# A fp32 Hymba layer on one core: four sums split as one buffer, six more seven-product quads, and output rows finished one pair later

## The chip, the cores and the metric

The kernel runs on one core of a Trainium2 chip. The metric is device time in microseconds (us) of one execution. The kernel before takes 1720.13 us, the median of 3 runs (1720.1 to 1720.97). Engines are named as the profile names them: PE does matrix products, DVE and ACT work on vectors, SP issues most transfers; PEld is PE's weight load and POOL is almost unused.

## The reference

`x` is 256 tokens by 4096, everything is fp32, and there is one layer.

```python
u = rmsnorm(x, norm_gain)
q, k, v, z_a, hc, b_gate, c_gate, z_c = split(u @ w_in)      # 8 x 2048 columns
attn = moba_attention(q, k, v, rel_bias) * silu(z_a)         # 16 heads of 128, causal;
                                # 256 tokens are one block, so each token sees its own block
conv = b_gate * short_conv(c_gate * hc, conv_w) * silu(z_c)  # causal, width 3
h = x + concatenate([attn, conv]) @ w_out                    # 4096 x 4096
return rmsnorm(h, final_gain)
```

## The kernel before, in words

**Pairs and quads.** The columns of `w_in` (16384) and `w_out` (4096) are cut into chunks of 512. Two chunks make a pair: pairs 0 to 15 are the input projection, 16 to 19 the output projection. The 4096 rows that a pair sums over are cut into 16 quads of 256 rows. A quad is one 1 MB tile `raw` (128 x 2048: two row blocks times two chunks), used with two token tiles of 128.

**Exact products.** Each fp32 operand is split in a high part (a cast on ACT, L540) and a low part (a subtraction on DVE, L542). A block of 128 x 128 x 512 is three matmuls: L607 and L608 (both parts of `x` with `hi`) and L610 (the high part of `x` with `lo`).

**Eight or seven products.** A plain quad is 8 blocks, 24 matmuls, and its `hi` and `lo` are split from `raw` directly. A "seven" quad uses a Strassen-like scheme of 7 blocks, 21 matmuls. For it DVE first adds blocks of weights into a tile `sum` (L521 1024 wide, L522 and L523 512 wide). Three blocks are split from `raw` (1536 wide), four from `sum` (two units of 1024). The operand of such a quad has 7 parts (8 for quad 14) rather than 4, so its `x` must be summed too (L150 to L152). How many sevens a pair has is given by a letter in `KIND` and, for pairs 0, 1 and 16, by a set. In all 141 of the 320 quads are sevens.

**Order of issue.** The units of all quads (one for a plain quad, three for a seven) are walked in order. Ahead of the matmuls of unit u the splits of unit u+2 are issued (`split`), and with the first unit of a quad the load of the quad two ahead. `hi` and `lo` have 3 buffers each, `raw` has 3. Each engine runs its instructions in the order of issue. So a DVE instruction that waits holds up all splits behind it.

**Accumulators.** Seven of the eight PSUM banks are in use in a pair: 1, 5, 6 and 7 belong to sevens alone and are added together after the last seven quad (`early`, `out_early`); 2, 3, 4 and 8 run to the end of the pair and are finished in `two_done` or `out_end`. In output pairs `out_early` adds into the residual rows `hg` at once, and `out_end` adds the rest, squares it on ACT and multiplies by the final gain `gf`, per 512 columns. In pairs 10, 12 and 14 the short convolution (`conv`) runs between the matmuls behind the last seven quad; it turns tiles on PE and sums on DVE.

**The end.** In pair 19 the `hi` and `lo` of the last three quads are kept, so that token tile 0 (banks 4 and 8) is finished first. `finish(0)` scales and stores it while PE works on banks 3 and 2 of token tile 1; `finish(1)` follows.

**The start.** Twelve matmuls on zeros (`WARM`) fill PE until the first operands are there.

Of the kernel before, what the change touches and what calls it, by code (L numbers as in the profile page):

```python
# [17 lines left out]
P = 128  # L18
# [12 lines left out]
WARM = 12  # L31
# [3 lines left out]
KIND = "01888888" "8n7n7n7n" "077e"  # L35
RING = 3
SLOT = 4
LO = 4
HI = 2
TS = (5, 7, 9, 11)  # L40
# [19 lines left out]
FIRST = (1, 3, 5, 7, 0, 9, 2, 11, 4, 8, 6, 10, 13, 12, 14, 15)  # L60
USUAL = tuple(range(16))
# [18 lines left out]
def of(pattern):  # L80
# [9 lines left out]
RAISE = {(1, 1): 4, (1, 3): 6, (1, 12): 0, (1, 13): 2, (1, 15): 14,  # L90
# [8 lines left out]
def hymba_layer(ctx: ExitStack, tc: tile.TileContext, xT, xres, gain, w, convw, wout,  # L99
# [15 lines left out]
    ss = const.tile([P, 2, 2 * NDP], F32, name="ss")  # L115
# [54 lines left out]
    def x_parts(q, xr):  # L170
        dst = operands(q)
        if q in SEVENS[0]:
            c = x_scaled(q, xr)
            sums_of(c)
            parts(dst, c[:, :7])
            return
# [12 lines left out]
    def m_parts(q, c):  # L189
        dst = operands(q)  # L190
        if q in SEVENS[N_PAIRS]:
            sums_of(c)
            parts(dst, c[:, :7])
        else:
            parts(dst[:, :4], c[:, :4])

    def made_up(q, c):
        sums_of(c)
        parts(A[q][:, 4:7], c[:, 4:7])
        g = 7 if q == BOTH else 0  # L200
        parts(A[q][:, g:g + 1], c[:, :1])
# [8 lines left out]
    def rsqrt(dst, ps, n):  # L210
# [6 lines left out]
        nc.vector.tensor_tensor(s, dst, dst, ALU.mult)  # L217
        nc.vector.tensor_tensor(s, s, v, ALU.mult)
# [122 lines left out]
    def conv(k, n):  # L341
# [8 lines left out]
        y = cur["pool"].tile([P, S], F32, name="y", bufs=2)  # L350
# [9 lines left out]
    ENDS = ((3, 1, 1, "v"), (2, 1, 0, "e"), (4, 0, 0, "u"), (8, 0, 1, "w"))  # L360

    def early(acc):

        e, v, u, w_ = (ep.tile([P, B], F32, name=f"e{i}") for i in range(4))
        nc.scalar.copy(e, acc[1])
        nc.vector.tensor_tensor(v, acc[6], e, ALU.add)  # L366
        nc.vector.tensor_tensor(u, acc[7], v, ALU.add)
        nc.vector.tensor_tensor(v, acc[5], v, ALU.subtract)
        nc.vector.tensor_tensor(w_, acc[5], u, ALU.subtract)
        return {"e": e, "v": v, "u": u, "w": w_}  # L370

    def scaled(es, rows):

        for _, t, n, name in ENDS:
            nc.scalar.activation(es[name], es[name], AF.Copy, scale=rows[n][:, t:t + 1])
# [52 lines left out]
    def row_of(p, t, n):  # L428
        c = 2 * p + n
        return fin["hg"][:, t, c * B:(c + 1) * B]  # L430

    def out_early(p, acc):
        v, u = (ep.tile([P, B], F32, name=f"e{i}") for i in range(2))
        x11, x12, x21, x22 = row_of(p, 1, 0), row_of(p, 1, 1), row_of(p, 0, 0), row_of(p, 0, 1)
        nc.scalar.copy(v, acc[1])
        nc.vector.tensor_tensor(x11, x11, v, ALU.add)
        nc.vector.tensor_tensor(v, acc[6], v, ALU.add)
        nc.vector.tensor_tensor(u, acc[7], v, ALU.add)
        nc.vector.tensor_tensor(v, acc[5], v, ALU.subtract)
        nc.vector.tensor_tensor(x12, x12, v, ALU.add)  # L440
        nc.vector.tensor_tensor(x21, x21, u, ALU.add)
        nc.vector.tensor_tensor(u, acc[5], u, ALU.subtract)
        nc.vector.tensor_tensor(x22, x22, u, ALU.add)
        gain_load(p)

    def out_end(p, ts=(1, 0), accs=(2, 3, 4, 8)):
        for b_, t, n, _ in ENDS:
            if t not in ts or b_ not in accs:
                continue
            hh = row_of(p, t, n)  # L450
            nc.vector.tensor_tensor(hh, cur["acc"][b_], hh, ALU.add)  # L451
            sq = ep.tile([P, B], F32, name=f"e{2 + n}")
            nc.scalar.activation(sq, hh, AF.Square, accum_out=ss[:, t, 2 * p + n:2 * p + n + 1])  # L453
            nc.vector.tensor_tensor(hh, hh, fin["gf"][:, n * B:(n + 1) * B], ALU.mult)  # L454

    def finish(t):
# [16 lines left out]
    def load(n):  # L473
# [33 lines left out]
    def split(u):  # L507
# [28 lines left out]
        step = B if n < LEAD else m if m < 4 * B else LO * B  # L536
# [9 lines left out]
    def tasks_of(p):  # L546
# [207 lines left out]
```

## Time and profile before

| | before |
|---|---|
| median of 3 runs | 1720.13 us |
| the profiled execution's own time | 1719.89 us |
| its span | 1718.1 us |
| mean granted clock of PE | 0.997 of full speed |
| PE busy | 1701.9 us (99%), 7639 matmuls |
| DVE busy | 1532.2 us (89%), 1534 instructions |
| ACT busy | 1014.3 us (59%), 1152 instructions |
| mean transfer rate | 216 GB/s |

The span is what the profiler covers from the first to the last event of the core; the 1.8 us between it and the execution's time lie outside. Matmuls overlap in the pipeline, so one matmul's own duration (about 0.39 us) is longer than the distance from one start to the next (about 0.23 us); the distance is what a matmul costs. A row of the timeline gives the start, the duration, the engine and line, output and input tiles with their shapes, how many instructions are put together, and in brackets how long the engine stood idle before and what it waited for.

### The profile page before, as it was taken

To read this page: it belongs to the slowest core of one execution; us is meant where nothing else is said; L and a number is where in the kernel's file an instruction comes from. 1 tells how busy PE (TensorE), PEld (TensorE's weight loads), DVE (VectorE), ACT (ScalarE), POOL (GpSimd) and SP (SyncE) were. 2 spreads that over 40 slices of the span, in tenths; PEclk is the share of its full clock that TensorE was granted. 3 is DMA by queue.
4 is the path that set the end of the run, shared out by engine and by line. 5 is a ranking of instruction groups with operands and counts; after the bars stand their busy time and mean duration, and the time that the engine had idled before them with its cause. 6 is when DMAs were issued, how large, how long until landed. Compare 5 with 4: busy or idle time off the path is not lost.

```text
span 1718.1 us, 20350 instructions
## 1 busy us (share of the span) xinstructions
PE 1701.9 (99%) x7639; PEld 1402.2 (82%) x7639; DVE 1532.2 (89%) x1534; ACT 1014.3 (59%) x1152; POOL 0.7 (0%) x6
## 2 busy tenths in 40 slices
PE   9999999999999999999999999999999999999996
PEld 7888888888888888888888888888888888888885
DVE  6889889898989898988998989898989989989897
ACT  6856665676567555755565555545556645555553
POOL 0000000000000000000000000000000000000000
PEclk9999999999999999999999999999999999999998
DMA  9875555555555555556555555555556777555554
GB/s 353 275 258 223 173 210 210 199 194 200 208 202 191 208 204 202 181 219 221 199 196 214 198 211 219 220 187 208 184 223 221 267 289 265 211 215 208 196 196 171
DMA packets 66703, 370.53 MB, mean 216 GB/s; under 512 B 8971, under 2 KB 13868, under 8 KB 25900
## 3 DMA queue, kind: packets, MB, share of 16 engines
q1 hardware_dynamic: 66316, 369.08, 58.6%
q8 instruction: 60, 0.98, 0.2%
q14 instruction: 39, 0.32, 0.1%
q10 hardware_dynamic: 288, 0.15, 0.0%
HBM read 360.02 MB, written 9.18 MB: 215 GB/s over the span
## 4 chain that ended last, share of the span: by engine, by line
PE 94%; DVE 4%; issue 1%; ACT 0%; DVEq 0%; ACTq 0%
PE p L607 31%; PE p L608 31%; PE p L610 30%; DVE lo L542 1%; PE p L275 0%; DVE hg L454 0%; PE p L268 0%; DVE y L353 0%; DVE sum L521 0%; PE p L292 0%; PE p L136 0%; ACT hi L540 0%; DVE hg L466 0%; PE p L303 0%; PE p L302 0%
## 5 line engine op out<-in xcount | busy, mean ns | idle before, releaser
L607 PE MATMUL p<-hi,k 128*128 128x512 f32 x2395 | 933.6, 391 | 1.8 <-DVE mt L355 1.1
L608 PE MATMUL p<-hi,k 128*128 128x512 f32 x2395 | 932.5, 390 | 0.0
L542 DVE TENSOR_TENSOR lo<-raw,hi 128x2048 fp32r<-128x2048 f32 (+2 forms) x323 | 644.1, 2013 | 66.3 <-PE p L610 37.0
L610 PE MATMUL p<-lo,k 128*128 128x512 f32 x2395 | 701.1, 392 | 0.0
L540 ACT CAST hi<-raw 128x1024 fp32r<-128x1024 f32 (+2 forms) x497 | 550.7, 1165 | 236.5 <-PE p L608 197.9
L607 PEld LDWEIGHTS p<-hi,k 128*128 128x128 f32 x2395 | 449.5, 188 | 99.8 <-ACT hi L540 3.6
L608 PEld LDWEIGHTS p<-hi,k 128*128 128x128 f32 x2395 | 449.6, 188 | 92.9 <-issue 0.6
L610 PEld LDWEIGHTS p<-lo,k 128*128 128x128 f32 x2395 | 446.8, 188 | 91.2 <-DVE lo L542 1.5
L540 ACT CAST hi<-sum 128x1024 fp32r<-128x1024 f32 x282 | 296.3, 1051 | 370.6 <-PE p L608 263.5
L542 DVE TENSOR_TENSOR lo<-sum,hi 128x1024 fp32r<-128x1024 f32 x282 | 342.6, 1221 | 82.8 <-PE p L610 74.3
L521 DVE TENSOR_TENSOR sum<-raw 128x1024 f32<-128x1024 f32 x141 | 171.9, 1219 | 4.5 <-DMA raw<-in_w_dram 3.9
L522 DVE TENSOR_TENSOR sum<-sum,raw 128x512 f32<-128x512 f32 x141 | 97.1, 688 | 2.5
L523 DVE TENSOR_TENSOR sum<-sum,raw 128x512 f32<-128x512 f32 x141 | 96.9, 687 | 1.8
L378 ACT ACTIVATE e<-e,rT 128x512 f32<-128x512 f32 x56 | 37.7, 716 | 21.8 <-DVE e L366 11.3
L155 ACT CAST k<-c 128x512 fp32r<-128x512 f32 (+3 forms) x37 | 20.1, 567 | 16.4 <-DVE c L152 9.1
L156 DVE TENSOR_TENSOR k<-c,k 128x512 fp32r<-128x512 f32 (+3 forms) x37 | 22.6, 622 | 5.1 <-ACT k L155 4.7
L453 ACT ACTIVATE e<-hg 128x512 f32<-128x512 f32 x16 | 10.0, 624 | 10.2 <-DVE hg L451 8.6
L152 DVE TENSOR_TENSOR c<-c 128x128 f32<-128x128 f32 x60 | 15.0, 286 | 0.7 <-DMA c<-m_d 0.5
L353 DVE SCALAR_TENSOR_TENSOR y<-p,cw,y 128x255 f32<-128x255 f32 (+1 forms) x32 | 14.7, 475 | 1.0 <-ACT y L351 1.0
L283 ACT ACTIVATE lg<-lg,st 128x256 f32<-128x256 f32 (+1 forms) x32 | 14.3, 448 | 1.8 <-DVE st L282 1.7
L181 DVE SCALAR_TENSOR_TENSOR k<-xr,g_sb,k 128x256 fp32r<-128x256 f32 x26 | 11.6, 476 | 4.1 <-ACT k L180 4.1
L454 DVE TENSOR_TENSOR hg<-hg,c 128x512 f32<-128x512 f32 x16 | 10.7, 689 | 2.8 <-ACT e L453 2.8
(110 smaller groups left out, 485.0 us busy)
## 6 DMA issues: line engine op xcount, KB each, us to landing
raw<-in_w_dram SPq DMA_DIRECT2D x254, 1024.0 KB, 5.0
raw<-in_wout_dram SPq DMA_DIRECT2D x64, 1024.0 KB, 4.9
xr<-in_xT_dram SPq DMA_DIRECT2D x20, 256.0 KB, 6.3
c<-m_d SPq DMA_DIRECT2D x20, 256.0 KB, 3.6
xq<-in_xres_dram SPq DMA_DIRECT2D x8, 512.0 KB, 4.9
hg<-in_xres_dram SPq DMA_DIRECT2D x4, 1024.0 KB, 6.5
out_dram<-hg SPq DMA_DIRECT2D x6, 512.0 KB, 3.9
raw<-in_w_dram SPq DMA_DIRECT2D x8, 256.0 KB, 5.5
```

The lines of the kernel that those rows point to most:

```text
L152: nc.vector.tensor_tensor(c[:, dst], c[:, a], c[:, b], op)
L155: nc.scalar.copy(dst[:, :, 0], c)
L156: nc.vector.tensor_tensor(dst[:, :, 1], c, dst[:, :, 0].bitcast(F32), ALU.subtract)
L378: nc.scalar.activation(e, e, AF.Copy, scale=r)
L521: nc.vector.tensor_tensor(t[:, :2], raw[:, 1:3], raw[:, :1].to_broadcast([P, 2, B]), ALU.add)
L522: nc.vector.tensor_tensor(t[:, 2], t[:, 0], raw[:, 2], ALU.add)
L523: nc.vector.tensor_tensor(t[:, 3], t[:, 2], raw[:, 3], ALU.add)
L540: nc.scalar.copy(hi[:, b:b + half], src[:, b:b + half])
L542: nc.vector.tensor_tensor(lo[:, c], src[:, c], hi[:, c].bitcast(F32), ALU.subtract)
L607: nc.tensor.matmul(acc[b_], a, h_, start=s0, stop=False)
L608: nc.tensor.matmul(acc[b_], b, h_, start=False, stop=False)
L610: nc.tensor.matmul(acc[b_], a, l_, start=False, stop=s1)
```

## The change

- **Sevens.** Pairs 0, 1, 10, 12, 14 and 16 each get one more seven quad: 147 rather than 141. The orders of pairs 0, 1 and 16 are written anew. The second operands of quads 4 and 6 are made up in pair 1 as before; quad 14 is a seven from pair 0 on, so its extra load in pair 1 goes.
- **One unit of four sums.** The four blocks split from `sum` are one unit in one `hi`/`lo` buffer, split in two pieces of 1024 (`LOS`). A seven quad is two units rather than three.
- **Early sums.** `early` makes its four tiles as one tile `es` with three DVE additions rather than four. At the last seven quad the look-ahead split is issued behind it.
- **Output rows.** `out_early` is now `early`. `out_end` only adds the four accumulators into `es`. Adding to the residual, squaring and multiplying by the gain are 1024 wide and are issued between the products of the next pair (`OUT_AT`). In the last pair the residual is added in `out_early`; the gain of the last 1024 columns is applied in `finish`, together with the scale.
- **First loads.** The first chunk of `raw` goes ahead of the first half of `xr` on SP's queue. `WARM` is 10.
- **Small ones.** `rsqrt` has one DVE step fewer, `y` has 4 buffers rather than 2, and the square-root table is fetched through `es`.

Counts of instructions, before and after: matmuls of 128 x 512 on `lo` 2395 and 2389, on `hi` 4790 and 4778, on zeros 12 and 10; DVE `lo<-sum` 282 and 294, `lo<-raw` 1536 wide 141 and 147, 2048 wide 174 and 168.

Three places show how the order on DVE moves. The first is DVE at the boundary of output pairs 17 and 18, before (`e`, `hg`, `p` and `c` are the early tiles, the residual rows, accumulators and the gain):

```order
L437 TENSOR_TENSOR e_11799<-p_11375,e_11799 128x512
L521 TENSOR_TENSOR sum<-raw 128x1024
L438 TENSOR_TENSOR e_11800<-p_11361,e_11799 128x512
L522 TENSOR_TENSOR sum<-sum,raw 128x512
L439 TENSOR_TENSOR e_11799<-p_11357,e_11799 128x512
L441 TENSOR_TENSOR hg<-hg,e_11800 128x512
L440 TENSOR_TENSOR hg<-hg,e_11799 128x512
L442 TENSOR_TENSOR e_11800<-p_11357,e_11800 128x512
L523 TENSOR_TENSOR sum<-sum,raw 128x512
L443 TENSOR_TENSOR hg<-hg,e_11800 128x512
L542 TENSOR_TENSOR lo<-raw,hi 128x1536
L451 TENSOR_TENSOR hg<-p_11308,hg 128x512
```

And the same place now:

```order
L372 TENSOR_TENSOR es<-p_11076,es 128x512
L529 TENSOR_TENSOR sum<-raw 128x1024
L373 TENSOR_TENSOR es<-p_11073,es 128x2x512
L530 TENSOR_TENSOR sum<-sum,raw 128x512
L550 TENSOR_TENSOR lo<-raw,hi 128x1536
L531 TENSOR_TENSOR sum<-sum,raw 128x512
L444 TENSOR_TENSOR es<-p_11018,es 128x512
L444 TENSOR_TENSOR es<-p_11024,es 128x512
L444 TENSOR_TENSOR es<-p_11027,es 128x512
L444 TENSOR_TENSOR es<-p_11021,es 128x512
L550 TENSOR_TENSOR lo<-sum,hi 128x1024 x2
L447 TENSOR_TENSOR hg<-hg,es 128x1024
```

The four additions into `hg` and the products with the gain no longer stand between the splits at the boundary; they come singly behind them.

The second place is DVE at the start of pair 11, from the first low part of that pair on, before:

```order
L542 TENSOR_TENSOR lo<-raw,hi 128x2048
L521 TENSOR_TENSOR sum<-raw 128x1024
L542 TENSOR_TENSOR lo<-raw,hi 128x1536
L522 TENSOR_TENSOR sum<-sum,raw 128x512
L542 TENSOR_TENSOR lo<-sum,hi 128x1024
L523 TENSOR_TENSOR sum<-sum,raw 128x512
L521 TENSOR_TENSOR sum<-raw 128x1024
L542 TENSOR_TENSOR lo<-sum,hi 128x1024
```

And now:

```order
L550 TENSOR_TENSOR lo<-raw,hi 128x2048
L529 TENSOR_TENSOR sum<-raw 128x1024
L550 TENSOR_TENSOR lo<-raw,hi 128x1536
L530 TENSOR_TENSOR sum<-sum,raw 128x512
L550 TENSOR_TENSOR lo<-sum,hi 128x1024
L531 TENSOR_TENSOR sum<-sum,raw 128x512
L550 TENSOR_TENSOR lo<-raw,hi 128x2048
L550 TENSOR_TENSOR lo<-sum,hi 128x1024
```

The second half of the low part of `sum` now stands behind a 2048-wide low part of the quad after it.

The third place is DVE at the end of the program, in `finish(0)` and what follows (`rf` is the row scale), before:

```order
L220 TENSOR_TENSOR rf<-rf,rs_s 128x1
L466 TENSOR_SCALAR hg<-hg,rf 128x512 x2
L466 TENSOR_SCALAR hg<-hg,rf 128x1024 x2
L451 TENSOR_TENSOR hg<-p_12495,hg 128x512
L454 TENSOR_TENSOR hg<-hg,c 128x512
L458 TENSOR_REDUCE s_13084<-ss 128x1
```

And now:

```order
L225 TENSOR_TENSOR rf<-rf,rs_s 128x1
L474 TENSOR_SCALAR hg<-hg,rf 128x512 x2
L474 TENSOR_SCALAR hg<-hg,rf 128x1024
L472 SCALAR_TENSOR_TENSOR hg<-hg,rf,c 128x1024
L459 TENSOR_TENSOR hg<-p_12148,hg 128x512
L459 TENSOR_TENSOR hg<-p_12154,hg 128x512
L464 TENSOR_REDUCE s_12720<-ss 128x1
```

The product with the gain (L454) is gone from the chain; the last 1024 columns are scaled by an instruction with a second tensor, and both additions of token tile 1 stand behind the scaling of tile 0.

```diff
-WARM = 12
+WARM = 10
-KIND = "01888888" "8n7n7n7n" "077e"
+KIND = "01888888" "8n8n8n8n" "077e"
+LOS = 2
+OUT_AT = (12, 18, 20, 26, 30, 40)
...
-ORDERS, SEVENS = zip(*([(FIRST, {8, 10, 12}), (USUAL, {4, 6, 8, 10, 12})]
+ORDERS, SEVENS = zip(*([(FIRST, {8, 10, 12, 14}), (SECOND, {4, 6, 8, 10, 12, 14})]
...
-                       + [(FIRST, {8, 10, 12})] + [of(PATS[k]) for k in KIND[N_PAIRS + 1:]]))
+                       + [(FIRST, {8, 10, 12, 14})] + [of(PATS[k]) for k in KIND[N_PAIRS + 1:]]))
...
-        nc.vector.tensor_tensor(s, dst, dst, ALU.mult)
-        nc.vector.tensor_tensor(s, s, v, ALU.mult)
+        for i in range(n):
+            nc.vector.scalar_tensor_tensor(s[:, i:i + 1], dst[:, i:i + 1], v[:, i:i + 1], dst[:, i:i + 1],
+                                           op0=ALU.mult, op1=ALU.mult)
...
+        es = cur["es"] = ep.tile([P, 4, B], F32, name="es")
+        nc.scalar.copy(es[:, 0], acc[1])
+        nc.vector.tensor_tensor(es[:, 1], acc[6], es[:, 0], ALU.add)
+        nc.vector.tensor_tensor(es[:, 2], acc[7], es[:, 1], ALU.add)
+        nc.vector.tensor_tensor(es[:, 1::2], acc[5][:, None, :].to_broadcast([P, 2, B]), es[:, 1:3], ALU.subtract)
...
+    def out_end(p):
+        for b_, t, n in ENDS:
+            nc.vector.tensor_tensor(part(t, n), cur["acc"][b_], part(t, n), ALU.add)
+    def added(p, t):
+        nc.vector.tensor_tensor(row_of(p, t), row_of(p, t), pair_of(t), ALU.add)
+    def squared(p, t):
+        nc.scalar.activation(pair_of(t), row_of(p, t), AF.Square, accum_out=ss[:, t, p:p + 1])
+    def gained(p, t):
+        nc.vector.tensor_tensor(row_of(p, t), row_of(p, t), fin["gf"], ALU.mult)
...
+            elif n == 4:
+                nc.vector.scalar_tensor_tensor(row, row, rf, fin["gf"], op0=ALU.mult, op1=ALU.mult)
...
-                for j, engine in enumerate((nc.sync, nc.scalar)):
-                    engine.dma_start(xr[:, j], xT[q][:, j * S:(j + 1) * S])
+                nc.scalar.dma_start(xr[:, 1], xT[q][:, S:])
...
+                if n == 0 and j == 0:
+                    nc.sync.dma_start(xrs[q][:, 0], xT[q][:, :S])
...
-                    (n, "sum", 0, (((4, 5),), ((7 if q == BOTH else 0, 7),))),
-                    (n, "sum", 2, (((5, 6),), ((2, 4),)))]
+                    (n, "sum", 0, (((4, 5),), ((g_at(q), 7),), ((5, 6),), ((2, 4),)))]
```

## Rows read from the trace of the kernel before

**Rows 1.** The page's first part: engine, busy us (share), number of instructions

```profile
PE 1701.9 (99%) x7639; PEld 1402.2 (82%) x7639; DVE 1532.2 (89%) x1534; ACT 1014.3 (59%) x1152; POOL 0.7 (0%) x6
```

**Rows 2.** Waits of PE: engine, line, waited for: us, times, longest

```profile
PE p L607 <- DVE mt L355: 1.1, 3, 0.4
PE p L607 <- ACT hi L540: 0.6, 2, 0.4
```

**Rows 3.** The chain that ended last, in pair 0: start, us, what

```profile
27.80 1.81 PE p L610 x8
```

**Rows 4.** Groups by line and shape: busy us, mean ns, idle before

```profile
L542 DVE TENSOR_TENSOR lo<-raw,hi 128x2048 fp32r<-128x2048 f32 x174 | 396.2, 2286 | 53.7 <-PE p L610 37.0 <-ACT hi L540 16.2
L542 DVE TENSOR_TENSOR lo<-sum,hi 128x1024 fp32r<-128x1024 f32 x282 | 342.6, 1221 | 82.8 <-PE p L610 74.3 <-ACT hi L540 7.0 <-ACT k L155 0.6
L542 DVE TENSOR_TENSOR lo<-raw,hi 128x1536 fp32r<-128x1536 f32 x141 | 247.0, 1752 | 11.8 <-ACT hi L540 11.8
L521 DVE TENSOR_TENSOR sum<-raw 128x1024 f32<-128x1024 f32 x141 | 171.9, 1219 | 4.5 <-DMA raw<-in_w_dram 3.9
L522 DVE TENSOR_TENSOR sum<-sum,raw 128x512 f32<-128x512 f32 x141 | 97.1, 688 | 2.5
L523 DVE TENSOR_TENSOR sum<-sum,raw 128x512 f32<-128x512 f32 x141 | 96.9, 687 | 1.8
```

**Rows 5.** Timeline of PE and DVE at the end of pair 10

```profile
953.82 0.63 PE L610 MATMUL p<-lo,k 128*128 128x512 f32 x2
954.83 0.47 PE L607 MATMUL p<-hi,k 128*128 128x512 f32 x1 [0.38 <-DVE mt L355]
...
954.27 0.41 DVE L355 TENSOR_TENSOR mt<-p,y 128x256 f32<-128x256 f32 x1
```

**Rows 6.** Windows: us, busy (x) of each engine, clock, DMA share, GB/s

```profile
877.00:955.00 78.00, 77.62 (x351) 63.90 (x350) 70.23 (x64) 44.01 (x47) 0.00 (x0) 1.00 0.56 204
```

**Rows 7.** Timeline of PE and ACT at the start of pair 19

```profile
1640.26 0.39 PE L610 MATMUL p<-lo,k 128*128 128x512 f32 x1
1641.08 0.50 PE L607 MATMUL p<-hi,k 128*128 128x512 f32 x1 [0.43 <-ACT hi L540]
...
1639.98 1.05 ACT L540 CAST hi<-sum 128x1024 fp32r<-128x1024 f32 x1 [3.25 <-DVE sum L523]
```

**Rows 8.** Timeline of PE and ACT at the start of the program

```profile
1.19 5.11 PE L136 MATMUL p<-zero 128*128 128x512 bf16 x12 [1.19 <-DVE tab L235]
6.29 0.50 PE L607 MATMUL p<-hi,k 128*128 128x512 f32 x1
...
5.22 0.51 ACT L180 ACTIVATE k<-xr,g_sb 128x256 fp32r<-128x256 f32 x1 [1.58 <-DMA xr<-in_xT_dram]
5.64 1.13 ACT L540 CAST hi<-raw 128x512 fp32r<-128x512 f32 x2
```

**Rows 9.** Timeline of PE, DVE and SP's queue at the end

```profile
1704.52 0.39 PE L610 MATMUL p<-k,k 128*128 128x512 f32 x1
...
1704.25 2.21 DVE L466 TENSOR_SCALAR hg<-hg,rf 128x512 f32<-128x512 f32 x4
1706.37 0.68 DVE L451 TENSOR_TENSOR hg<-p,hg 128x512 f32<-128x512 f32 x1
1707.90 0.69 DVE L454 TENSOR_TENSOR hg<-hg,c 128x512 f32<-128x512 f32 x1 [0.85 <-ACT e L453]
1709.32 0.16 DVE L217 TENSOR_TENSOR rs_s<-rf 128x1 f32<-128x1 f32 x1
1710.10 2.21 DVE L466 TENSOR_SCALAR hg<-hg,rf 128x512 f32<-128x512 f32 x4
...
1704.76 8.85 SPq L467 DMA_DIRECT2D out_dram<-hg  x10
```

**Rows 10.** Windows at the end, with Rows 6' columns

```profile
1705.00:1712.00 7.00, 0.00 (x0) 0.00 (x0) 5.67 (x16) 2.47 (x5) 0.00 (x0) 0.80 0.85 329
1712.00:1718.00 6.00, 0.00 (x0) 0.00 (x0) 0.30 (x1) 0.00 (x0) 0.00 (x0) 0.50 0.81 315
```

More of the change, by code (lines that the diff above doesn't have):

```diff
@@ L114, in hymba_layer @@
     sx = const.tile([P, 2, NDP], F32, name="sx")
-    ss = const.tile([P, 2, 2 * NDP], F32, name="ss")
+    ss = const.tile([P, 2, NDP + 1], F32, name="ss")
     const.tile([P, 8], F32, name="pad")
@@ L142, in hymba_layer, with g_at @@
     A = {}
+    def g_at(q):
+        return 7 if q == BOTH else 0
     def operands(q):
@@ L191, in m_parts @@
         if q in SEVENS[N_PAIRS]:
-            sums_of(c)
-            parts(dst, c[:, :7])
+            sums_of(q, c)
+            parts(dst, c[:, :SIZES[q]])
         else:
@@ L197, in made_up @@
     def made_up(q, c):
-        sums_of(c)
+        sums_of(q, c)
         parts(A[q][:, 4:7], c[:, 4:7])
-        g = 7 if q == BOTH else 0
-        parts(A[q][:, g:g + 1], c[:, :1])
+        parts(A[q][:, g_at(q):g_at(q) + 1], c[:, g_at(q):g_at(q) + 1])
     def squares(n):
@@ L349, in conv @@
             nc.tensor.transpose(ps[:, S + t * P:S + (t + 1) * P], b[:, t], ident)
-        y = cur["pool"].tile([P, S], F32, name="y", bufs=2)
+        y = cur["pool"].tile([P, S], F32, name="y", bufs=4)
         nc.scalar.activation(y, ps[:, :S], AF.Copy, scale=cw[:, k, 2:3])
@@ L356, in conv, with part @@
         m_store(16 + k)
-    ENDS = ((3, 1, 1, "v"), (2, 1, 0, "e"), (4, 0, 0, "u"), (8, 0, 1, "w"))
+    ENDS = ((3, 1, 1), (2, 1, 0), (4, 0, 0), (8, 0, 1))
     def early(acc):
[L364 to L375, printed above, removed]
+        es = cur["es"] = ep.tile([P, 4, B], F32, name="es")
[3 more added lines that the diff above has]
+        nc.vector.tensor_tensor(es[:, 1::2], acc[5][:, None, :].to_broadcast([P, 2, B]), es[:, 1:3], ALU.subtract)
+    def part(t, n):
+        return cur["es"][:, 2 * (1 - t) + n]
     def scaled(e, r):
@@ L380, in two_done @@
     def two_done(dsts, rows):
-        acc, es = cur["acc"], cur["es"]
-        for b_, t, n, name in ENDS:
-            nc.vector.scalar_tensor_tensor(dsts[n][:, t], acc[b_], rows[n][:, t:t + 1], es[name],
+        for b_, t, n in ENDS:
+            nc.vector.scalar_tensor_tensor(dsts[n][:, t], cur["acc"][b_], rows[n][:, t:t + 1], part(t, n),
                                            op0=ALU.mult, op1=ALU.add)
@@ L426, in gain_load, with row_of, pair_of @@
                                       ap=[[0, P], [1, 2 * B]]))
-    def row_of(p, t, n):
-        c = 2 * p + n
-        return fin["hg"][:, t, c * B:(c + 1) * B]
+    def row_of(p, t):
+        return fin["hg"][:, t, 2 * p * B:2 * (p + 1) * B]
+    def pair_of(t):
+        return cur["es"][:, 2 * (1 - t):2 * (2 - t)].rearrange("p n c -> p (n c)")
     def out_early(p, acc):
[L433 to L443, printed above, removed]
-        gain_load(p)
@@ L446, in out_end @@
[L446 to L454, printed above, removed]
+        early(acc)
@@ new lines, in out_early @@
+        if p == NDP - 1:
+            for t in (0, 1):
+                added(p, t)
+        gain_load(p)
+    def out_end(p):
+        for b_, t, n in ENDS:
+            nc.vector.tensor_tensor(part(t, n), cur["acc"][b_], part(t, n), ALU.add)
[5 more added lines that the diff above has]
+        nc.vector.tensor_tensor(row_of(p, t), row_of(p, t), fin["gf"], ALU.mult)
@@ L456, in finish, with last_end @@
+    def last_end(t, accs):
+        for b_, t_, n in ENDS:
+            if t_ == t and b_ in accs:
+                row = row_of(NDP - 1, t)[:, n * B:(n + 1) * B]
+                nc.vector.tensor_tensor(row, cur["acc"][b_], row, ALU.add)
+                nc.scalar.activation(part(t, n), row, AF.Square, accum_out=ss[:, t, NDP - 1 + n:NDP + n])
     def finish(t):
@@ L614, in hymba_layer @@
         p, i, q = quads[n]
-        if u + 2 < len(units):
-            split(u + 2)
         cur["p"] = p
@@ L619, in hymba_layer @@
         end_of_quad = u + 1 == len(units) or units[u + 1][0] != n
+        early_now = end_of_quad and i == last_seven[p]
+        if u + 2 < len(units) and not early_now:
+            split(u + 2)
         if start_of_quad and i == 0:
@@ L657, in hymba_layer @@
             if p < N_PAIRS:
-                es = cur["es"] = early(acc)
+                early(acc)
                 rows = (rQ if p < 8 and p % 2 == 0 else rT, rT)
-                for j, (_, t, c, name) in enumerate(ENDS):
-                    tasks.setdefault(TS[j] if i < NQ - 2 else 4 + j, []).append((scaled, (es[name], rows[c][:, t:t + 1])))
+                for j, (_, t, c) in enumerate(ENDS):
+                    tasks.setdefault(TS[j] if i < NQ - 2 else 4 + j, []).append((scaled, (part(t, c), rows[c][:, t:t + 1])))
             else:
                 out_early(p - N_PAIRS, acc)
+            split(u + 2)
         if (p, i) in M_AT:
@@ L684, in hymba_layer @@
                 out_end(p - N_PAIRS)
-    out_end(NDP - 1, (0,))
+    last_end(0, (4, 8))
     finish(0)
```

26 lines of the change are left out of this document (16 added, 10 removed).

## The prediction

> **What bounds the kernel now.** I read the page's first part, then PE's waits, then the timeline at the few places where PE does wait, and last the two ends of the program. The first part is to show that PE is busy for 1701.9 us of the span of 1718.1 and that DVE follows with 1532.2 [rows 1]. PE's waits are to show that almost nothing is left between its matmuls: 1.1 us in three places behind the convolution (L355) and 0.6 us in two behind a cast [rows 2]. So in the middle of the program time is the number of matmuls times the distance from one to the next, and that distance is read from a stretch with no wait: eight L610 in 1.81 us, 0.2267 us each [rows 3]. Whatever else can be won lies in the ends and in those few waits, and what can be lost lies with DVE, whose splits must be ready in time.
>
> The two ends are to be seen as chains of other engines. At the start the first real matmul is issued at 6.29 us, right behind twelve matmuls on zeros [rows 8]. At the end the last matmul is issued at 1704.52 and ends at 1704.91, and the span ends 13.2 us later [rows 9].
>
> **Matmuls.** Six quads go from 8 products to 7: 6 x 3 = 18 matmuls fewer, 18 x 0.2267 = -4.1 us [rows 3]. All lie on the path. The price is on DVE. A seven quad costs it 1.75 + 2 x 1.22 + 1.22 + 0.69 + 0.69 = 6.8 us by the means, a plain one 2.29 [rows 4], so each new seven adds 4.5 us, 27 us in all against 186 us in which DVE is idle now (1718.1 - 1532.2). The cover must hold in the pair itself: in a stretch of 78 us of pair 10, one of those that get a seven, DVE works 70.2 us, so 7.8 are idle [rows 6]; less 4.5, and less the 0.7 us by which the pair gets shorter, 2.6 remain. That is thin, and it is the first rival's ground.
>
> **One unit of four sums.** The work is the same. What changes is the look-ahead: two units ahead now reaches nearly a quad further where sevens follow each other, by about one half unit of 6 matmuls, 1.4 us. Splits are issued that much earlier, which pays where PE waits now. But on DVE a 2048-wide low part of the next quad comes to stand ahead of the second half of the low part of `sum`, in eight places (two in pairs 0 and 1, the others at the starts of pairs 10 to 15). No row shows such a wait. From below it is nothing: the low parts are needed last in a unit, behind eight matmuls of 0.23 us, and have been ready before that in most places. From above it is the whole instruction, 2.29 us [rows 4], eight times, 18 us. I take 0.2 us each, near the lower end, since the waits of PE name no `lo` at all now [rows 2]: +1.5.
>
> **Ends of pairs 10, 12 and 14.** PE's next matmul comes 954.83 - 954.05 = 0.78 us after the one before (the second of the two that start at 953.82), 0.55 more than the pace, because the last tile of the convolution came late from DVE, its sum at 954.27 [rows 5]. Three such places, with the slower refill behind each about 1.9 us. With splits 1.4 us earlier, four `y` buffers and one DVE instruction fewer in `early`, I take 1.5 of them as gone. Bounds: 0 (the new seven takes the slack) and 1.9.
>
> **Output pairs.** At the start of pair 19 PE waits 1641.08 - 1640.26 - 0.23 = 0.59 us for a cast, and that cast had waited 3.25 us for DVE's last addition of `sum` [rows 7]. DVE was late because at the boundary it had sixteen instructions of 0.69 us in the way (eight in `out_early`, four additions and four products in `out_end`). Seven remain there, three of `early` and four additions; the others come later, singly. Reading starts in the same way over all output pairs gives 2.3 us beyond the pace, this place being the widest. I take -2.0; bounds 0 and -2.3. The twelve wide instructions that were moved (two additions and two products with the gain for each of three pairs) are about 1.2 us each, priced by L521 [rows 4]; DVE's idle time between splits hides them. Without it each would cost its 1.2 us, 15 us in all, which I count as nothing because they stand behind a split, not ahead of one.
>
> **Pair 1.** Quads 4 and 6 get their made-up operands while the new order runs plain quads in between; ACT now scales `x` between two halves of one cast. I take +0.4, the bounds are 0 and 4 us (one cast that waits for a whole quad of 21 matmuls).
>
> **First loads.** Between start and first matmul there are twelve matmuls on zeros, 5.11 / 12 = 0.426 us each [rows 8]. Two fewer bring the end of that stretch to 5.45. The first real operand was late too: ACT waited 1.58 us for the second half of `xr` until 5.22 and only then cast the first `hi`, at 5.64 [rows 8]. The new order casts it ahead of that. So the first matmul can come at about 5.5: -0.8. Bounds: +1.5, if the first operands come later than now, and -1.1.
>
> The Trainium skill, "DMA: Bandwidth & Descriptors", section "Issuing engines are not separate DMA queues", speaks against this edit: SP's and ACT's transfers share the same 16 engines, so putting one half of `xr` on the other queue makes nothing land sooner, and the chunk put ahead delays the half behind it. The trace agrees as far as the half on ACT's queue was the one that came last. By that rule the term would be about 0; it is the fourth rival.
>
> **The end.** Now the addition of bank 2 stands behind the scaling of token tile 0: it starts at 1706.37, 1.46 us after the last matmul's end at 1704.91 [rows 9]. In the new order both tiles' chains are shorter and bank 4 and 8 are left 36 matmuls ahead of the end, so tile 0 is scaled by about the time of the last matmul and the addition waits for PE alone: -1.4. The product with the gain, 0.69 us from 1707.90, leaves the chain: -0.6 at its distance. One of four steps between 1709.32 and 1710.10 goes, (1710.10 - 1709.32) / 4 = -0.2 [rows 9]. The last columns need a second tensor, which is slower: an instruction with two tensors of 1024 takes 1.22 us [rows 4], the four here 2.21 together [rows 9]. I take no cost, since the transfers end last: after 1712 DVE works only 0.3 us more, and they move 315 GB/s until the end [rows 10]. Uncovered it would be +0.5. Sum -2.2; bounds -2.4 and 0.
>
> **The sum**, against the profiled execution's 1719.89: -4.1 - 2.2 - 2.0 - 1.5 - 0.8 + 1.5 + 0.4 = -8.7, that is 1711.2. The median of the runs is 0.24 above that execution, so 1711.4.
>
> **The rivals.**
>
> First, DVE is the bound in the pairs with a new seven. For it: 2.6 us of idle time in such a stretch [rows 6] are less than the waits that the convolution makes. Against: DVE's idle time before a low part is mostly waiting for PE to free a buffer (74.3 of 82.8 us [rows 4]), which a queue that is behind doesn't have. Then the waits at the ends of pairs 10, 12 and 14 stay (+1.5) and each grows by some 0.8 us (+2.5): 1715.4.
>
> Second, only the matmuls count: the waits are made up of something else, and the stores at the end are bound by transfers, so that an earlier start gains nothing. Then 1720.13 - 4.1 = 1716.0. Against it: the transfers of tile 1 can't begin before their scaling at 1710.10 [rows 9].
>
> Third, the other side: the low part of `sum` behind the 2048-wide one is late in all eight places. PE then waits there up to 2.29 us; with the 1.5 that I have counted taken out, 1709.9 + 8 x 2.29 = 1728.2. It decides from (1723.6 - 1709.9) / 8 = 1.7 us each on, three quarters of the instruction. Against it: PE never waits for `lo` in the rows [rows 2], and there are eight matmuls of high parts, 1.8 us, ahead of the first low one.
>
> Fourth, the first loads gain nothing because the transfers share the engines, or PE's first real matmuls run slower than now: they are 0.43 us apart on zeros against 0.23 later, and a lower pace for a few more of them gives back what two fewer saved. 1712.2.
>
> **How the numbers follow.** About 0.2%, 3.4 us, is what a measurement can tell from no change here. I give my forecast 0.62 (1708 to 1714), the first rival 0.18, the second 0.06, the third 0.04 and the fourth 0.10. Faster by over 0.2% means below 1716.7: the forecast, the fourth, most of the first (0.15) and half of the second: 0.90. Within it 0.06, the rest of those two. Slower 0.04, the third. The range of 1707.0 to 1717.0 takes in all bounds that help (another 1.9 us: 0.4 + 0.3 + 0.3 + 0.2, and 0.7 of the waits that I added) with some room, and on the upper side the first, second and fourth rivals; what it leaves out is the third and the far ends.
>
> **What the profile after would show.** Matmuls: L610's successor counts 2389 and the pace stays at 0.2267. Sums: the waits of PE name no `lo`; if they do, at the starts of pairs 10 to 15, the third rival speaks. Convolution: the three waits for L355's successor are gone or under 0.1 us; if they grow, the first. Output pairs: no wait of PE for a cast. Start: the first real matmul at about 5.5 us; later than 6.3 is the fourth. End: the addition of bank 2 starts within 0.1 us of the last matmul's end, and the span ends 11 us after that end. I would be wrong if DVE's idle time in pairs 10, 12 and 14 vanished with waits of PE behind it.

## The result and the profile after

The changed kernel takes 1708.84 us, the median of 6 runs (1708.36 to 1709.75); the kernel before, beside it, 1720.12 us, also of 6 runs. The ratio is 0.9935, with a 95% interval of 0.9922 to 0.9948. It is 11.3 us faster, where 8.7 were forecast. The profiled execution takes 1708.57 us, and its span is 1706.7 us.

The page's first part answers to [rows 1]; the second row is the only wait of PE that is left behind its first instructions (columns as in [rows 2]):

```profile
PE 1693.4 (99%) x7619; PEld 1399.6 (82%) x7619; DVE 1549.2 (91%) x1525; ACT 1035.2 (61%) x1144; POOL 0.7 (0%) x6
```

```profile
PE p L622 <- ACT k L185: 0.9, 1, 0.9
```

PE works 8.5 us less. DVE works 17 us more and is now at 91%, and yet PE never waits for it: both kinds of wait in [rows 2] are gone, and the one that is listed belongs to the start of the program.

The start of each pair on PE, read from the timelines of both kernels, says where the time went. The six pairs with a new seven have 3 matmuls fewer each.

| stretch | after against before, us | of it matmuls | rest |
|---|---|---|---|
| until the first real matmul (6.29 to 5.95) | -0.35 | | -0.35 |
| pairs 0 and 1 | -1.00 | -1.36 | +0.36 |
| pairs 2 to 9 | -0.71 | | -0.71 |
| pairs 10 to 15 | -4.15 | -2.04 | -2.11 |
| pair 16 | -0.55 | -0.68 | +0.13 |
| pairs 17 to 19 | -2.59 | | -2.59 |
| behind the last matmul (13.2 to 11.1) | -2.10 | | -2.10 |
| span | -11.45 | -4.08 | -7.37 |

Where pair 11 begins, PE before, then PE and DVE now, to be held against [rows 5]:

```profile
952.89 0.40 PE L607 MATMUL p<-hi,k 128*128 128x512 f32 x1
...
949.38 0.93 PE L625 MATMUL p<-lo,k 128*128 128x512 f32 x3
950.15 0.40 PE L622 MATMUL p<-hi,k 128*128 128x512 f32 x1
...
949.77 0.41 DVE L360 TENSOR_TENSOR mt<-p,y 128x256 f32<-128x256 f32 x1
```

Pair 11 began at 952.89 us and now begins at 950.15. The tile that PE waited for is the second of the pair's four, not the last as the prediction says: two more follow, at 955.64 and 958.07 before and at 950.89 and 952.27 now. Its sum began 1.4 us behind pair 11's first matmul (954.27) and now begins 0.4 us ahead of it (949.77), and the gap of 0.78 us between matmuls is gone.

DVE's low parts from `sum`, which carried most of DVE's idle time before [rows 4]:

```profile
L550 DVE TENSOR_TENSOR lo<-sum,hi 128x1024 fp32r<-128x1024 f32 x294 | 351.0, 1219 | 7.6 <-ACT hi L548 5.6
```

The 74.3 us in which DVE stood still there until PE had freed a buffer are gone. That does not mean that the waiting has ended. The waits of all low parts and of ACT's casts, two rows before and then three now:

```profile
DVE lo L542 <- PE p L610: 111.3, 89, 2.9
DVE lo L542 <- ACT hi L540: 35.8, 36, 3.1
...
DVE lo L550 <- ACT hi L548: 99.4, 81, 4.2
DVE lo L550 <- PE p L625: 11.5, 14, 1.6
ACT hi L548 <- PE p L623: 358.2, 268, 4.0
```

DVE hardly waits for PE any more, but it waits 99.4 us for ACT's casts, and those still wait 358.2 us for PE (461.4 before). It is still PE that paces both engines, now through ACT.

The start of the program, PE and ACT, answers to [rows 8]:

```profile
1.19 3.90 PE L138 MATMUL p<-zero 128*128 128x512 bf16 x10 [1.19 <-DVE tab L240]
5.95 0.51 PE L622 MATMUL p<-hi,k 128*128 128x512 f32 x1 [0.86 <-ACT k L185]
...
4.72 0.62 ACT L548 CAST hi<-raw 128x512 fp32r<-128x512 f32 x1 [1.58 <-DMA raw<-in_w_dram]
5.38 0.91 ACT L185 ACTIVATE k<-xr,g_sb 128x256 fp32r<-128x256 f32 x2
```

The zeros end at 5.09 us, where 5.45 was forecast; the last ones of this execution come faster than 0.43 us apart (see the last section). The first operand from `x` now stands behind the cast, and PE waits 0.86 us for it. The first half of `xr`, issued at 1.19 us, landed only 4.1 us later, at 5.3:

```profile
xr<-in_xT_dram SPq DMA_DIRECT2D x1, 128.0 KB, 4.1
```

The end, PE and DVE, answers to [rows 9], and the window behind it to [rows 10]:

```profile
1695.17 0.39 PE L625 MATMUL p<-k,k 128*128 128x512 f32 x1
...
1695.59 0.69 DVE L459 TENSOR_TENSOR hg<-p,hg 128x512 f32<-128x512 f32 x1 [1.88 <-PE p L625]
1698.59 1.55 DVE L474 TENSOR_SCALAR hg<-hg,rf 128x512 f32<-128x512 f32 x3
1700.04 1.28 DVE L472 SCALAR_TENSOR_TENSOR hg<-hg,rf,c 128x1024 f32<-128x1024 f32 x1
```

```profile
1701.00:1706.00 5.00, 0.00 (x0) 0.00 (x0) 0.33 (x1) 0.00 (x0) 0.00 (x0) 0.50 0.86 339
```

The last addition waits for PE alone and starts 0.04 us behind the last matmul's end (1695.56). Scaling of token tile 1 begins 3.0 us behind that end, where it began 5.2 us behind it (1710.10 - 1704.91). The instruction with the second tensor is 1.28 us long, and after 1701.3 only transfers are left.

### The profile page after: what moved, and what is told of

Read it like the earlier page. It is cut to its first block, busy times and chain, and to the rows that moved or that the text cites. A ratio compares the mean times of both kernels' runs of the same rounds, so it can differ in the third digit from the quotient of the medians.

```text
span 1706.7 us, 20017 instructions
## 1 busy us (share of the span) xinstructions
PE 1693.4 (99%) x7619; PEld 1399.6 (82%) x7619; DVE 1549.2 (91%) x1525; ACT 1035.2 (61%) x1144; POOL 0.7 (0%) x6
## 4 chain that ended last, share of the span: by engine, by line
PE 99%; DVE 0%; DMA 0%; ACT 0%; issue 0%; DVEq 0%; ACTq 0%
PE p L625 32%; PE p L623 32%; PE p L622 32%; PE p L280 0%; PE p L273 0%; PE p L297 0%; DMA raw<-in_w_dram 0%; PE p L307 0%; PE p L308 0%; PE p L306 0%; PE p L281 0%; PE p L332 0%; PE p L354 0%; PE p L352 0%; DVE hg L472 0%; DVE hg L474 0%
## 5 line engine op out<-in xcount | busy, mean ns | idle before, releaser
L548 ACT CAST hi<-raw 128x1024 fp32r<-128x1024 f32 (+2 forms) x491 | 563.6, 1175 | 372.7 <-PE p L623 220.3
L625 PE MATMUL p<-lo,k 128*128 128x512 f32 x2389 | 641.3, 392 | 0.0
L550 DVE TENSOR_TENSOR lo<-sum,hi 128x1024 fp32r<-128x1024 f32 x294 | 351.0, 1219 | 7.6 <-ACT hi L548 5.6
L529 DVE TENSOR_TENSOR sum<-raw 128x1024 f32<-128x1024 f32 x147 | 179.3, 1220 | 18.0 <-DMA raw<-in_w_dram 15.9
L530 DVE TENSOR_TENSOR sum<-sum,raw 128x512 f32<-128x512 f32 x147 | 100.9, 687 | 1.5
L531 DVE TENSOR_TENSOR sum<-sum,raw 128x512 f32<-128x512 f32 x147 | 100.9, 686 | 1.2
L379 ACT ACTIVATE es<-es,rT 128x512 f32<-128x512 f32 x56 | 38.4, 720 | 35.3 <-DVE es L373 18.4
L161 DVE TENSOR_TENSOR k<-c,k 128x512 fp32r<-128x512 f32 (+4 forms) x36 | 23.2, 663 | 1.6 <-ACT k L160 1.5
L373 DVE TENSOR_TENSOR es<-p,es 128x1024 f32<-128x1024 f32 x20 | 24.4, 1218 | 0.0
L160 ACT CAST k<-c 128x512 fp32r<-128x512 f32 (+4 forms) x36 | 20.8, 601 | 5.5 <-DVE c L157 4.3
L372 DVE TENSOR_TENSOR es<-p,es 128x512 f32<-128x512 f32 x20 | 13.7, 684 | 0.0
L371 DVE TENSOR_TENSOR es<-p,es 128x512 f32<-128x512 f32 x20 | 13.7, 684 | 0.0
```

The source lines that it names most:

```text
L160: nc.scalar.copy(dst[:, :, 0], c)
L161: nc.vector.tensor_tensor(dst[:, :, 1], c, dst[:, :, 0].bitcast(F32), ALU.subtract)
L373: nc.vector.tensor_tensor(es[:, 1::2], acc[5][:, None, :].to_broadcast([P, 2, B]), es[:, 1:3], ALU.subtract)
L379: nc.scalar.activation(e, e, AF.Copy, scale=r)
L529: nc.vector.tensor_tensor(t[:, :2], raw[:, 1:3], raw[:, :1].to_broadcast([P, 2, B]), ALU.add)
L530: nc.vector.tensor_tensor(t[:, 2], t[:, 0], raw[:, 2], ALU.add)
```

## The experiments

The theory at first was: the matmuls give their 4.1 us because the longer look-ahead of the one unit hides DVE's extra work; the same look-ahead takes the waits behind the convolution away; the shorter work at the boundary takes away those of the output pairs. The rivals: DVE pays for the sevens somewhere; `y` or the early sums removed the convolution's waits; the look-ahead alone removed those of the output pairs. The runs are the changed kernel with one edit, or two where it is said; two runs edit the kernel before. "End" is the end of the last matmul against that of the changed kernel, read from the traces, since the times of one kernel differ by up to 2.7 us from run to run. Each run has one trace, and in it pairs that the edit does not touch mostly agree within 0.2 us; twice, as is said below, they differ by 0.5 to 0.7.

### The sevens: put back, and put into the kernel before

```diff
-KIND = "01888888" "8n8n8n8n" "077e"
+KIND = "01888888" "8n7n7n7n" "077e"
```

(and the orders and sets of pairs 0, 1 and 16 as before)

> The changed kernel with the sevens, their pairs and orders of the kernel before (141 of them, 18 matmuls more). If the new sevens give what their matmuls take and nothing is paid for them: 18 x 0.2267 = 4.1 us above the changed kernel, about 1712.9, with PE again without waits behind its first matmul. If DVE's extra work (4.5 us for each seven) costs waits in the changed kernel that the trace hides, the difference is smaller, 2 to 3 us. If the orders of pairs 0, 1 and 16 matter for themselves, the starts of pairs 1, 2 and 17 move by more or less than 0.68 us for each three matmuls.

1713.12 us (5 runs), end +5.15. Of this 4.08 are the 18 matmuls. The rest is 0.2 in pairs 0 and 1 (0.4 and -0.2) and 0.9 in pair 2, which belong to the old orders of pairs 0 and 1. One of the places in pair 2 is this:

```profile
183.19 0.39 PE L622 MATMUL p<-hi,k 128*128 128x512 f32 x1
183.98 0.47 PE L622 MATMUL p<-hi,k 128*128 128x512 f32 x1 [0.41 <-DVE lg L283]
```

In pairs 10 to 15 the difference is 2.07, which is 9 matmuls and nothing else. So the sevens of pairs 10, 12 and 14 are paid for nowhere in the changed kernel. The other way round, the kernel before with the new `KIND` alone (three sevens more, in pairs 10, 12 and 14):

> The kernel before with one more seven in pairs 10, 12 and 14 and nothing else (9 matmuls fewer, -2.0 us by themselves). If the pairs had room on DVE as they were, the time is 1718.1 and the waits behind the convolution stay at 0.55 us each. If DVE is behind there without the longer look-ahead, the waits at the ends of these pairs grow by 1 us or more each, and the time is 1719.5 to 1723.

1721.29 us (11 runs) against 1720.47, ratio 1.0005 (0.9996 to 1.0013): the 9 matmuls gave nothing. The last matmul ends 1.5 us later than before, so 3.6 us of new waits stand against them, 3.0 in pairs 10 to 15 and 0.7 in pair 19, which the edit does not touch. PE's waits and, of its timeline, the place where one begins:

```profile
PE p L607 <- ACT hi L540: 2.2, 6, 0.8
PE p L607 <- DVE mt L355: 1.1, 3, 0.4
```

```profile
891.40 0.84 PE L610 MATMUL p<-lo,k 128*128 128x512 f32 x3
892.70 0.50 PE L607 MATMUL p<-hi,k 128*128 128x512 f32 x1 [0.46 <-ACT hi L540]
```

Without the rest of the change the sevens are worth nothing there. The convolution's waits have not grown; the new ones lie earlier in the pair, where two sevens follow each other.

### The look-ahead

```diff
-(n, "sum", 0, (((4, 5),), ((g_at(q), 7),), ((5, 6),), ((2, 4),)))]
+(n, "sum", 0, (((4, 5),), ((g_at(q), 7),))),
+(n, "sum", 2, (((5, 6),), ((2, 4),)))]
```

> The changed kernel with the four sums of a seven quad split as two units of two again. If the longer look-ahead removed the waits at the ends of pairs 10, 12 and 14, they come back, and larger than before (0.55 us each), since these pairs now have one seven more: 2 to 6 us above the changed kernel, 1711 to 1715. If the four buffers of y or the shorter early sums removed them, no wait comes back: within 0.5 us of the changed kernel. In pairs 2 to 9, where the changed kernel gained 0.7 us without fewer matmuls, the first theory expects these 0.7 us to go too, since only the order of the products of a seven quad was changed there.

1712.88 us (5 runs), end +3.90: 1.2 in pairs 2 to 9, 2.8 in pairs 10 to 15, 0.1 in the output pairs. PE and ACT at the same place in pair 10, DVE's last addition of `sum` there, the cast at the same place in pair 12, and PE, PEld, DVE and ACT (columns as in [rows 6]) from the start of pair 10 to that wait, in this run and over the same stretch of the changed kernel:

```profile
890.39 0.84 PE L626 MATMUL p<-lo,k 128*128 128x512 f32 x3
891.67 0.50 PE L623 MATMUL p<-hi,k 128*128 128x512 f32 x1 [0.44 <-ACT hi L549]
...
890.57 1.05 ACT L549 CAST hi<-sum 128x1024 fp32r<-128x1024 f32 x1 [2.73 <-PE p L624]
889.76 0.70 DVE L532 TENSOR_TENSOR sum<-sum,raw 128x512 f32<-128x512 f32 x1
1056.74 1.05 ACT L549 CAST hi<-sum 128x1024 fp32r<-128x1024 f32 x1 [1.92 <-DVE sum L532]
```

```profile
867.70:892.00 24.30, 23.86 (x105) 19.37 (x104) 24.30 (x25) 15.66 (x16) 0.00 (x0) 1.00 0.48 173
866.65:890.95 24.30, 24.30 (x108) 20.00 (x107) 24.13 (x24) 16.88 (x17) 0.00 (x0) 1.00 0.53 186
```

PE waits for a cast of `sum`. In pair 10 the profile puts the wait of that cast down to PE, which freed the buffer three units back; but DVE's last addition ended at 890.46, only 0.1 us before the cast began. In pairs 12 and 14 the same cast waits for that addition. DVE works without a pause, 24.30 of 24.30 us, from the start of the pair to the wait: there it is the slower engine, as the first rival has it. In the changed kernel it is as full in that stretch (24.13 us), and PE does not wait. So what the one unit gives is the lead with which the splits enter the stretch. That the three buffers, filled with small units, cap this lead is argued, not shown: in this run DVE's low parts wait 57.1 us for PE in other places, in the changed kernel 11.5, and no run has a larger ring. The expectation was right in size (2 to 6 us) and wrong in place: no wait comes back behind the convolution. It also says that in pairs 2 to 9 only the order of products was changed; `early` was changed there too.

### The waits behind the convolution

```diff
-y = cur["pool"].tile([P, S], F32, name="y", bufs=4)
+y = cur["pool"].tile([P, S], F32, name="y", bufs=2)
```

> The changed kernel with two buffers for y rather than four. The run with two units of two sums showed no wait behind the convolution, so the longer look-ahead is not what took these waits away. If the y buffers did, three waits of about 0.55 us come back at the ends of pairs 10, 12 and 14, 1.7 us in all. If the shorter early sums, issued ahead of the split, did, none comes back.

One run: 1708.47 us, end -0.07, and no wait of PE beyond that at the start. The other way round, four buffers in the kernel before:

> The kernel before with four buffers for y rather than two. If the buffers alone set the waits behind the convolution, the three waits of 0.55 us go and the last matmul ends 1.7 to 1.9 us earlier. If DVE was late there for other reasons, they stay.

One run: 1720.05 us, and the waits stand as they were:

```profile
PE p L607 <- DVE mt L355: 1.1, 3, 0.4
```

So neither the look-ahead nor the buffers are needed to keep these 1.9 us away, the buffers alone are not enough, and the sevens have no part in it (the first two runs). What the run with two units still has is `early` with three additions rather than four, and the split that now stands behind it. The three take 2.6 us where the four took 2.7, so their number hardly counts. The order does: DVE at `early`'s first addition, in the kernel before, where pair 11 starts at 952.89, and with two units, where it starts at 951.90:

```profile
938.97 4.49 DVE L542 TENSOR_TENSOR lo<-raw,hi 128x2048 fp32r<-128x2048 f32 x2 [2.10 <-PE p L610]
943.38 0.68 DVE L366 TENSOR_TENSOR e<-p,e 128x512 f32<-128x512 f32 x1
...
938.01 2.29 DVE L551 TENSOR_TENSOR lo<-raw,hi 128x2048 fp32r<-128x2048 f32 x1 [2.10 <-ACT hi L549]
940.22 0.68 DVE L371 TENSOR_TENSOR es<-p,es 128x512 f32<-128x512 f32 x1
```

One 2048-wide low part fewer stands ahead of it, and `early` begins 11.7 us ahead of the next pair rather than 9.5. This speaks for the split's place; no run tried it alone, nor the one unit with the old `early`, so whether the look-ahead would have been enough by itself stays open.

### The output pairs

```diff
-OUT_AT = (12, 18, 20, 26, 30, 40)
+OUT_AT = (1, 2, 3, 4, 5, 6)
```

> The changed kernel with the residual additions, squares and gain products of an output pair issued behind the first six products of the next pair, rather than behind 12 to 40. If the burst of DVE work at the boundary caused the waits in the output pairs, they come back, at the starts of pairs 17, 18 and 19: PE waits for a cast or a low part, about 2 us in all, 1710 to 1711. If the longer look-ahead alone removed them, nothing changes: within 0.5 us of 1708.8, and PE shows no wait there.

1708.69 us (5 runs), end -0.06, no wait in the output pairs. Beside the one unit it does not matter where this work stands. Both edits at once (two units, and `OUT_AT` early):

> The changed kernel with two units of two sums and the output work behind the first six products of the next pair: neither the longer look-ahead nor the late place. If either of the two alone keeps PE from waiting in the output pairs, the waits come back only now: about 2 us more than the run with two units alone, at the starts of pairs 17, 18 and 19. If what counts is that 16 instructions at the boundary became 7 and the rest wide ones, none comes back, and the end is where it was with two units.

One run: 1714.45 us, end +5.86, that is 2.0 more than with two units alone, 1.1 of it in the output pairs. PE and ACT in pair 17:

```profile
1471.76 0.40 PE L626 MATMUL p<-lo,k 128*128 128x512 f32 x1
1472.61 0.50 PE L623 MATMUL p<-hi,k 128*128 128x512 f32 x1 [0.46 <-ACT hi L549]
...
1471.51 1.05 ACT L549 CAST hi<-sum 128x1024 fp32r<-128x1024 f32 x1 [2.96 <-DVE sum L532]
```

It is the chain of [rows 7] again: a cast waits for `sum`, behind the output work on DVE. So either edit alone keeps PE from waiting there, and it takes both undone to bring the waits back. Against the changed kernel pairs 17 to 19 are then 1.5 us longer, not the 2.6 that the whole change gained there; the other 1.1 belongs to something that no run undid (the fewer and wider instructions at the boundary are the candidate). Of the rest of the 2.0, 0.5 is a wait in pair 11, where this run and the one with two units alone have the same code; its cause stays open.

### The ends

The gain back in the last pair's end, one product behind each square, and plain scaling in `finish`:

```diff
+nc.vector.tensor_tensor(row, row, fin["gf"][:, n * B:(n + 1) * B], ALU.mult)
...
-            elif n == 4:
-                nc.vector.scalar_tensor_tensor(row, row, rf, fin["gf"], op0=ALU.mult, op1=ALU.mult)
```

> The changed kernel with the product with the gain of the last 1024 columns back in the last pair's end (one of 0.69 us behind each square), and a plain scaling in the last step. If the product was on the chain that ends the program: the last stores come 0.6 us later, the end of the span moves from 11.15 to 11.75 us behind the last matmul. If the stores are bound by the transfers of token tile 0 before them, the end does not move (under 0.1 us). Time 1709.4 or 1708.8; the trace tells them apart better than the time.

1709.26 us (5 runs). Scaling of token tile 1:

```profile
1699.15 2.21 DVE L473 TENSOR_SCALAR hg<-hg,rf 128x512 f32<-128x512 f32 x4
```

It begins 3.63 us behind the last matmul's end (1695.52) rather than 3.03, and the span ends 11.7 us behind it rather than 11.1: +0.6. The product was on the chain. The slower scaling is hidden by transfers: it ends at the same distance from the last matmul in both kernels, 5.8 us, and the span still ends 0.6 us earlier without the product.

The first half of `xr` first again:

```diff
+nc.sync.dma_start(xr[:, 0], xT[q][:, :S])
 nc.scalar.dma_start(xr[:, 1], xT[q][:, S:])
```

> The changed kernel with the first half of xr ahead of the first chunk of raw again. ACT then scales both halves of xr ahead of the first cast, as in the kernel before. If that order on ACT held up the first matmul, it starts later than 5.95 us, at 6.2 to 6.3, as before, and the time is 0.3 us above the changed kernel. If the chunk put ahead only delays the half of xr and nothing is won, the first matmul starts at 5.95 or before.

1709.03 us (5 runs); the first matmul starts at 6.43, end +0.34. The order on ACT was the reason, and putting the chunk first is worth 0.3 us. Then all first loads on SP, the second half of `xr` behind two chunks:

> The changed kernel with all first loads on SP in the order first half of xr, two chunks of raw, second half of xr, two chunks. The first products need only the first half of xr and the first chunk. If what came last was delayed by transfers beside it (the half on ACT's queue and the chunk ahead), both are there by 4.7 us, ACT casts right away and the first matmul starts at 5.4 to 5.6, right behind the zeros: 0.4 us below the changed kernel. If the first transfers take as long whatever goes beside them, it starts at 5.9 as in the changed kernel.

1708.37 us (5 runs, 1708.14 to 1708.55). The first matmul starts at 5.66, 0.29 earlier; at the start of pair 1 only 0.09 of it is left, at the end 0.01. The lead is lost between 10.5 and 13 us, where PE's weight load waits for low parts:

```profile
10.54 0.19 PEld L625 LDWEIGHTS p<-lo,k 128*128 128x128 f32 x1 [0.20 <-DVE lo L550]
12.09 0.19 PEld L625 LDWEIGHTS p<-lo,k 128*128 128x128 f32 x1 [0.32 <-DVE lo L550]
```

### A version that is faster than both

```diff
-KIND = "01888888" "8n8n8n8n" "077e"
+KIND = "01888888" "8n8n8n8n" "088e"
```

> The changed kernel with one more seven quad in each of the output pairs 17 and 18 (8 rather than 7). If DVE still has room there, 6 matmuls fewer give -1.36 us, 1707.5, and PE shows no wait. If DVE becomes the bound, waits for a cast or a low part come up at the starts of pairs 18 and 19, and the time is 1708.5 to 1711.

1707.62 us (5 runs, 1707.53 to 1708.0, all below the lowest of the changed kernel), ratio to the kernel before 0.9928 (0.9915 to 0.9941). Over pairs 17 and 18 the end gains 0.69, not 1.36. The rest is paid in one place of each pair (of two with this order). DVE there, in pair 17, and what PE's weight load waits for:

```profile
1505.47 2.28 DVE L550 TENSOR_TENSOR lo<-raw,hi 128x2048 fp32r<-128x2048 f32 x1
1507.67 1.22 DVE L550 TENSOR_TENSOR lo<-sum,hi 128x1024 fp32r<-128x1024 f32 x1
```

```profile
PEld p L625 <- DVE lo L550: 1.0, 3, 0.4
```

The second half of a low part stands behind a 2048-wide one: the third rival's mechanism, here at last, at 0.3 us in each pair. With the loads of the run before it as well:

> The changed kernel with one more seven in pairs 17 and 18 and with all first loads on SP in the order first half of xr, two chunks, second half of xr, two chunks. The two single runs ended 0.56 us and 0.01 us earlier at the last matmul; if they add up, 0.6 us below the changed kernel in the span, 1708 or a little less. If one more seven is all it gives, the same within 0.3 us as the run with the sevens alone.

1707.81 us (5 runs), ratio 0.9929 (0.9915 to 0.9942): the loads add nothing to the time. PE and ACT at its start:

```profile
5.37 0.80 PE L622 MATMUL p<-hi,k 128*128 128x512 f32 x1
5.97 0.63 PE L623 MATMUL p<-hi,k 128*128 128x512 f32 x1
6.39 0.63 PE L625 MATMUL p<-lo,k 128*128 128x512 f32 x1
6.82 0.55 PE L622 MATMUL p<-hi,k 128*128 128x512 f32 x1
7.21 0.39 PE L623 MATMUL p<-hi,k 128*128 128x512 f32 x1
...
3.19 0.51 ACT L185 ACTIVATE k<-xr,g_sb 128x256 fp32r<-128x256 f32 x1 [0.53 <-DMA g_sb<-in_gain_dram]
```

The operands are there 0.6 us earlier, but the next matmuls are 0.42 and 0.43 us apart, the zeros' distance; 0.23 is reached at 7.2 us. 512 columns in 0.427 us are 1.2 a nanosecond, the lower of PE's two levels, 1.2 GHz. The granted clock of the profile reads 1.00 in that stretch all the same, so this rests on the distance alone.

## Why the prediction was right, and where not

The sum was -8.7 us and the kernel gained 11.3. All the help that the prediction lists beyond its sum, 1.9 us, leads to 1709.5, and 1708.84 lies below that: it is in the range because of the room that was added. The terms, one by one:

**Matmuls: right**, -4.1 of -4.1, at no cost (first experiment). **The end: right**, -2.1 for -2.2. The gain weighed 0.6 for 0.6. **Output pairs: right in place**, -2.6 for -2.0, beyond the bound of -2.3. But the reason given is only a part of it: of 1.5 us the work that left the boundary is one of two sufficient causes and the look-ahead the other; the cause of the other 1.1 is not shown. **Pair 1: right**, +0.36 over pairs 0 and 1 for +0.4.

**The step that failed: "I take 0.2 us each ... +1.5"** for the low parts that are placed behind wider ones. The trace has seven such places, not eight (two in pair 1, one each in pairs 11 to 15; in pairs 12 and 14 one more stands behind a 1536-wide low part), and neither PE nor its weight load waits for a low part in any of them. The lower bound was the truth, and the argument for it stood in the same paragraph: the matmuls of high parts ahead of the first low one. In the version with two more sevens the same order costs 0.3 us in one of the two places of each of pairs 17 and 18. So the mechanism exists and its price is of the size that I took, but it was booked for places that cover it.

**The gain that was not seen:** pairs 2 to 9 gain 0.7 us without fewer matmuls, and splitting the one unit again takes 1.2 back there; something else in the change costs 0.5, most of it in pairs 2 and 3, and no run says what. In the changed kernel the one unit is worth 3.9 us, of which the prediction's sum had none as a gain of its own. It treated the unit as a risk, and booked what it hides under the matmuls.

**The convolution: right size, cause not the one given.** -2.0 in pairs 11, 13 and 15 for -1.5, put down to the look-ahead, the buffers and the instruction saved in `early`. The runs show that the first two are not needed and that the buffers alone are not enough; the traces point to the split's place behind `early`, which the prediction does not name.

**First loads: wrong by half**, -0.35 for -0.8. The chunk in front delayed the half of `xr`, and PE waited 0.86 us for it. The rule weighed there, of the Trainium skill, "DMA: Bandwidth & Descriptors", section "Issuing engines are not separate DMA queues", pointed the right way as to the half: put first, ACT scales it at 3.19 us (the last run); put behind the chunk, it lands at 5.3 and is scaled at 5.38. As to the term it did not: the chunk first is still 0.3 us better, because of the order on ACT. The other half of the fourth rival, a lower pace that gives the start back, is seen in the last run alone; in the one before it the lead is lost to low parts that come late.

**The first rival, DVE as the bound, fell in the changed kernel, and holds without the one unit**: in the kernel before the three sevens of pairs 10, 12 and 14 bring 3.0 us of waits, most of them from 23 us into the pair on, behind a stretch in which DVE is busy 24.30 of 24.30 us. The reserve of 2.6 us worked out over 78 us of pair 10 was not the quantity to look at: in the first 24 us of the pair DVE's idle time is at most 0.2 us in any of the kernels. What differs is the lead with which DVE enters them.

## What to carry to other kernels

Count look-ahead in the consumer's work, not in units: merging two small units of a ring of three was worth 3.9 us here, with the same three buffers. Idle time of a producer over the whole program is no room by itself: in the kernel before DVE waited 74.3 us for PE in one group of splits, and yet 9 matmuls' worth of sevens gained nothing there, because the stretch that took them had no idle time at all. Look for the stretch in which the producer never stops, and ask with what lead it enters. When two edits each remove a wait by themselves, undoing one shows nothing; undo both before saying which one did it.

## What was not expected of the hardware

Starting PE's real work earlier than about 6 us gained nothing that the times show. Of 0.57 and 0.29 us won at the first matmul (5.37 and 5.66 against 5.95), 0.11 and 0.09 were left when pair 1 began, and two traces of the same start (the changed kernel and the version with two more sevens) differ by 0.16 us in pair 0.

PE's step from the distance of the zeros to that of the later matmuls does not come at a fixed time. PE's weight loads become shorter with it. The changed kernel, on zeros, and the run with all first loads on SP:

```profile
4.15 0.15 PEld L138 LDWEIGHTS <-zero 128*128 128x128 bf16 x1 [0.28 <-issue]
4.49 0.10 PEld L138 LDWEIGHTS <-zero 128*128 128x128 bf16 x1 [0.20 <-issue]
...
5.82 0.31 PEld L623 LDWEIGHTS p<-hi,k 128*128 128x128 f32 x1
6.39 0.19 PEld L625 LDWEIGHTS p<-lo,k 128*128 128x128 f32 x1 [0.26 <-DVE lo L550]
```

It came by 4.5 us in the first, by 6.4 in the second and, by the distances shown above, by 7.2 in the last run, although the last two have the same code at their start, and all three have matmuls on zeros from 1.2 us on. So what an earlier first matmul gives depends on when that step comes in the execution at hand; one trace of each kernel can't tell what it would give on average.
